# The last norm of a trunk layer: roots one step ahead of the scaling, one quarter row on ScalarE and GpSimd

## The chip, the cores and the metric

The kernel runs on one core of a Trainium2 chip. The metric is the device time of one execution in microseconds (us), as the median of three runs. The engines are named as the profile names them: PE (TensorE matmul), PEld (its weight loads), DVE (VectorE), ACT (ScalarE), POOL (GpSimd) and SP (SyncE, which issues DMAs). A small q behind a name is the engine's sequencer: issues, waits, drains.

## The reference

One layer of an encoder trunk on 512 tokens of 1024 channels: a mixing sub-layer (recurrent branch, attention branch, merge, norm, residual), and a feed-forward sub-layer. Only the end of the second one matters here:

```python
def rms_norm(x, gain):
    y = xf * lax.rsqrt(jnp.mean(xf * xf, axis=-1, keepdims=True) + RMS_EPS)
    return y * gain
...
ffn_out = jnp.einsum("bsf,fd->bsd", jax.nn.gelu(gate) * val, w_down[layer])
x = x + rms_norm(ffn_out, ffn_norm_post[layer])
```

For each token: the sum of squares of its 1024 outputs of the down projection, the reciprocal root of it (the "factor"), and output = product with gain, times factor, plus residual.

## The kernel before

All matrix products are float32 made of two parts: each operand is cast to a high part (ScalarE) and the rest is its low part (VectorE, a subtraction of two operands in SBUF), and three matmuls multiply high by high, high by low and low by high.

**The down projection** is done as seven products of half-size blocks (a scheme with fewer products than eight). Each product n has six steps, so there are 42 steps, in the order of products 1, 4, 5, 6, 7, 3, 2. Step i does this, in an order that is written out by hand (`manual_schedule`, nothing is reordered by a planner; every engine takes its instructions in this order):

- `load_w(i + 5)`: SyncE loads the weights of a later step.
- `down_step(i)`: the matmuls of step i, for two tiles of 128 tokens (t = 0, 1) and 512 columns, into PSUM banks `slot[n][t]`.
- `prep(i + 2)`: the casts (ScalarE, `wh_dn` and `ah`) and splits (VectorE, `wl_dn` and `al`) for step i + 2, out of rings of four buffers.
- `extra[i]`: whatever else is put into that step, the last norm's work among it. `at_[n]` is the first step of product n: 30 for product 3, 36 for product 2.

**The tokens** are four tiles of 128 (t = 0 to 3). Tiles 2 and 3 need products that are complete after step 29; tiles 0 and 1 need all of them. The matmuls of the last four steps (38 to 41) are put behind all preparations, and go by tile: tile 0 for the four steps, then tile 1's columns 0 to 255 (`X`), then 256 to 511 (`Y`).

**The norm of tiles 2 and 3** stands in `extra` of the steps from 30 on. For each of the two halves of a row, one step folds the PSUM result with a kept partial sum (VectorE, `fold`, L1671), the next squares and sums it (ScalarE, `square`, L1678) and multiplies with the gain into `os[t]` (VectorE, `gained`, L1681). Then one step does both of these:

- `scale_of`: root on ScalarE (L269), reciprocal on VectorE (L271);
- `finish_by_dma`: ScalarE scales the whole row, 128x1024 (L1699), GpSimd issues a DMA that adds the residual (L1700, `accum_op`), and a DMA puts the row out (L1701), for tile 2 from GpSimd's queue, for tile 3 from SyncE's.

Tile 2 has the steps 30 to 34, tile 3 the steps 34 to 38. Step 38 is the first whose matmuls come late, so its `extra` runs behind all preparations.

**The norm of tiles 0 and 1** has its second half (columns 512 to 1023) folded, squared and multiplied in steps 38 and 39. The rest follows the last matmuls: `fold_part` (L1759, L1760: fold on VectorE, square on ScalarE), `gained_part` (L1763), `rest_end` (L263, which adds two of the partial sums of squares), and `finish` (L1694, L1696): VectorE computes scale times row plus residual in one instruction, and a DMA puts the piece out.

A DMA queue issues in order: SyncE's queue holds tile 3's output first, then the pieces of tiles 0 and 1.

Of the kernel before, what the change touches and what calls it, by code (L numbers as in the profile page):

```python
# [11 lines left out]
AF = mybir.ActivationFunctionType  # L12
ALU = mybir.AluOpType
# [84 lines left out]
def kernel(  # L98
# [15 lines left out]
    nc = tc.nc  # L114
    act, dve, pool, pe = nc.scalar, nc.vector, nc.gpsimd, nc.tensor
# [11 lines left out]
    ov = out.rearrange("(t p) d -> p t d", p=P)  # L127

    HALVES = (slice(0, 512), slice(512, 1024))
# [131 lines left out]
    def rest_of(name, parts, eps=EPS):  # L261
        rest = small.tile([P, 1], F32, tag="ss", name=f"rest_{name}")
        dve.tensor_scalar(out=rest, in0=parts[0], scalar1=eps, scalar2=parts[1] if len(parts) > 1 else None, op0=ALU.add,  # L263
                          **({"op1": ALU.add} if len(parts) > 1 else {}))
        return rest

    def rstd_of(part, name, rest=epst):
        sd = small.tile([P, 1], F32, tag="sd", name=f"sd_{name}")
        act.activation(out=sd, in_=part, func=AF.Sqrt, bias=rest)  # L269
        rs = small.tile([P, 1], F32, tag="rs", name=f"rs_{name}")  # L270
        dve.reciprocal(rs, sd)  # L271
        return rs
# [85 lines left out]
    X, Y = slice(0, SH), slice(SH, S)  # L358
# [172 lines left out]
    with ExitStack() as rg:  # L531
        rt, ixt, tt = {}, {}, {}
        last_act = [None]
        with ExitStack() as r0:
# [69 lines left out]
            with tc.tile_pool(name="pre", bufs=2, side="right", reuse_waits="tile") as pre, ExitStack() as wp:  # L604
# [80 lines left out]
                for c in HALVES:  # L685
                    pool.tensor_tensor(out=us[0].wl[:, c], in0=us[0].raw[:, c], in1=us[0].wh[:, c].bitcast(F32),
                                       op=ALU.subtract)
# [363 lines left out]
    with ExitStack() as at:  # L1051
# [165 lines left out]
        i = KD - 2  # L1217
# [37 lines left out]
    x2t = xpool.tile([P, NT, D], F32, name="x2t")  # L1255
# [323 lines left out]
    with man2:  # L1579
# [90 lines left out]
        def fold(i, t, ps):  # L1670
            dve.tensor_tensor(out=kept[i][t], in0=ps, in1=kept[i][t], op=ALU.add)  # L1671

        s2o = {t: dpool.tile([P, 3], F32, name=f"s2_o{t}", bufs=1) for t in range(NT)}
        os = [dpool.tile([P, D], F32, name=f"o{t}") for t in range(NT)]
        junk = dpool.tile([P, DH], F32, name="junk")

        def square(t, h, src):
            act.activation(out=junk, in_=src, func=AF.Square, scale=ROOT, accum_out=s2o[t][:, h : h + 1])  # L1678

        def gained(t, h, src):  # L1680
            dve.tensor_tensor(out=os[t][:, HALVES[h]], in0=src, in1=gpost[:, HALVES[h]], op=ALU.mult)  # L1681

        rso = {}
# [3 lines left out]
        def rest_end(t, *cols):  # L1687
            rest_o[t] = rest_of(f"o{t}", [s2o[t][:, i : i + 1] for i in cols])

        def scale_of(t, c=0):  # L1690
            rso[t] = rstd_of(s2o[t][:, c : c + 1], f"o{t}", rest_o[t])

        def finish(t, c, queue):
            dve.scalar_tensor_tensor(out=os[t][:, c], in0=os[t][:, c], scalar=rso[t], in1=x2t[:, t, c],  # L1694
                                     op0=ALU.mult, op1=ALU.add)
            queue.dma_start(ov[:, t, c], os[t][:, c])  # L1696

        def finish_by_dma(t, queue):
            act.activation(out=os[t], in_=os[t], func=AF.Copy, scale=rso[t])  # L1699
            nc.gpsimd.dma_start(os[t], x2d[t * P : (t + 1) * P], accum_op=ALU.add)  # L1700
            queue.dma_start(ov[:, t], os[t])  # L1701

        extra = {i: [] for i in range(len(STEPS))}
        at_ = {n: NS * PRODUCTS.index(n) for n in PRODUCTS}
# [18 lines left out]
        for t in range(2):  # L1723
            todo = []
            for h, n in ((1, 5), (0, 4)):
                todo += [lambda t=t, n=n: fold(n, t, slot[1][t]),
                         lambda t=t, h=h, n=n: (square(2 + t, h, kept[n][t]), gained(2 + t, h, kept[n][t])) + ((rest_end(2 + t, 1),) if h else ())]
            todo.append(lambda t=t: (scale_of(2 + t), finish_by_dma(2 + t, (nc.gpsimd, nc.sync)[t])))
            for i, f in enumerate(todo):
                extra[at_[3] + 4 * t + i].append(f)  # L1730
        for t in range(2):
            a = at_[2] + 2 + t
            extra[a].append(lambda t=t: fold(6, t, slot[5][t]))
# [24 lines left out]
        def fold_part(t, c, i):  # L1758
            dve.tensor_tensor(out=kept[1][t][:, c], in0=slot[2][t][c.start // SH][:, c] if t else slot[2][t], in1=kept[1][t][:, c], op=ALU.add)  # L1759
            act.activation(out=junk[:, c], in_=kept[1][t][:, c], func=AF.Square, scale=ROOT, accum_out=s2o[t][:, i : i + 1])  # L1760

        def gained_part(t, c):
            dve.tensor_tensor(out=os[t][:, c], in0=kept[1][t][:, c], in1=gpost[:, c], op=ALU.mult)  # L1763
# [3 lines left out]
        scale_of(0)  # L1767
        fold_part(1, X, 0)
        finish(0, HALVES[1], nc.sync)
        gained_part(1, X)  # L1770
        rest_end(1, 0, 1)
        fold_part(1, Y, 2)
        gained_part(1, Y)
        scale_of(1, 2)
        finish(0, HALVES[0], nc.sync)
        finish(1, HALVES[1], nc.sync)
        finish(1, X, act)
        finish(1, Y, nc.sync)


_INS = ["x", "gains", "cp", "w_in", "w_f", "rgw", "w_proj_a", "w_proj_b", "w_out", "w_up", "w_down"]
# [86 lines left out]
```

## Time and profile before

| what | before |
|---|---|
| median of three runs | 875.69 us (875.36 to 876.43) |
| profiled execution, its own time | 875.8 us |
| its span, first to last instruction | 873.9 us |
| granted TensorE clock, mean | 0.997 |
| last matmul starts, PE | 866.14 us |
| reciprocal of tile 1, DVE | 867.78 us |
| last output DMA issued, SP | 870.07 us |

The profiled execution's own time is 1.9 us more than its span. In a timeline row the first number is the start in us from the span's start, the second the duration; a row with x2 or more is several instructions that follow one another, merged, with the shape of the first. In square brackets stands how long the engine was idle before it, and what ended that wait. In a chain or a list of waits, "A <- B: total, times, longest" means that A waited for B. In a group's row, the numbers behind the bar are busy us and the mean ns of one.

### The profile page before, as it was taken

To read this page: it belongs to the slowest core of one execution; us is meant where nothing else is said; L and a number is where in the kernel's file an instruction comes from. 1 tells how busy PE (TensorE), PEld (TensorE's weight loads), DVE (VectorE), ACT (ScalarE), POOL (GpSimd) and SP (SyncE) were. 2 spreads that over 40 slices of the span, in tenths; PEclk is the share of its full clock that TensorE was granted. 3 is DMA by queue.
4 is the path that set the end of the run, shared out by engine and by line. 5 is a ranking of instruction groups with operands and counts; after the bars stand their busy time and mean duration, and the time that the engine had idled before them with its cause. 6 is when DMAs were issued, how large, how long until landed. Compare 5 with 4: busy or idle time off the path is not lost.

```text
span 873.9 us, 15792 instructions
## 1 busy us (share of the span) xinstructions
PE 864.5 (99%) x5856; PEld 793.1 (91%) x5856; DVE 734.8 (84%) x1209; ACT 598.9 (69%) x1031; POOL 229.7 (26%) x282
## 2 busy tenths in 40 slices
PE   9999999999999999999999999999999999999996
PEld 7888888888899998888888889999999999988885
DVE  7998469774578859999868699999999999889997
ACT  7556595543466657776755496888888888678664
POOL 4244534454111033323205100233233233100000
PEclk9999999999999999999999999999999999999998
DMA  7777689979965478354606662789999988699875
GB/s 267 227 252 215 203 218 251 268 205 246 229 164 151 121 233 286 111 175 153 230 26 205 220 212 100 148 208 248 260 241 257 230 212 216 209 392 353 299 224 159
DMA packets 72256, 188.38 MB, mean 216 GB/s; under 512 B 7601, under 2 KB 28129, under 8 KB 71794
## 3 DMA queue, kind: packets, MB, share of 16 engines
q1 hardware_dynamic: 48576, 130.86, 44.6%
q0 software_dynamic: 23456, 56.37, 30.3%
q8 instruction: 46, 0.75, 0.3%
q14 instruction: 32, 0.26, 0.1%
q10 hardware_dynamic: 146, 0.14, 0.1%
HBM read 152.79 MB, written 37.83 MB: 218 GB/s over the span
## 4 chain that ended last, share of the span: by engine, by line
PE 91%; DVE 5%; issue 2%; ACT 1%; DMA 0%; DVEq 0%; ACTq 0%
PE dn L1564 7%; PE up L459 7%; PE up L462 7%; PE up L460 7%; PE av L1133 2%; PE pa L242 2%; PE ga L244 2%; PE ga L243 2%; PE pa L244 2%; PE pa L243 2%; PE ga L242 2%; PE wo L1275 2%; PE pb L242 2%; PE xa L242 2%; PE wo L1276 2%
## 5 line engine op out<-in xcount | busy, mean ns | idle before, releaser
L1434 DVE SCALAR_TENSOR_TENSOR u<-up,cft,u 128x511 f32<-128x511 f32 x96 | 71.3, 745 | 3.5 <-ACT u L1428 1.8
L395 POOL DMA_DIRECT2D ml<-raw_up x42 | 36.1, 860 | 144.3 <-ACT ml L394 84.8
L459 PE MATMUL up<-sh,th 128*128 128x256 f32 x252 | 59.6, 275 | 0.2 <-DVE up L478 0.2
L460 PE MATMUL up<-sl,th 128*128 128x256 f32 x252 | 59.5, 275 | 0.0
L196 ACT CAST wh_dn<-raw_dn 128x1024 fp32r<-128x1024 f32 x42 | 43.9, 1045 | 17.8 <-DMA raw_dn<-td 12.3
L199 DVE TENSOR_TENSOR wl_dn<-raw_dn,wh_dn 128x1024 fp32r<-128x1024 f32 x42 | 51.1, 1217 | 4.7 <-ACT wh_dn L196 4.7
L355 DVE TENSOR_TENSOR tl<-t,th 128x1024 fp32r<-128x1024 f32 x42 | 51.3, 1221 | 0.0
L1428 ACT ACTIVATE u<-up,cft 128x512 f32<-128x512 f32 x48 | 37.0, 780 | 20.7 <-PE up L462 9.6
L459 PEld LDWEIGHTS up<-sh,th 128*128 128x128 f32 x252 | 48.4, 192 | 0.4 <-DVE up L478 0.4
L460 PEld LDWEIGHTS up<-sl,th 128*128 128x128 f32 x252 | 48.4, 192 | 0.0
L1442 POOL TENSOR_TENSOR yf<-u,u 128x512 f32<-128x512 f32 x23 | 30.7, 1333 | 61.7 <-issue 46.1
L441 ACT CAST th<-t 128x1024 fp32r<-128x1024 f32 x42 | 43.7, 1043 | 3.0 <-DVE t L355 0.7
L1564 PE MATMUL dn<-wh_dn,al 128*128 128x512 f32 (+1 forms) x180 | 45.0, 366 | 0.0
L1564 PE MATMUL dn<-wl_dn,ah 128*128 128x512 f32 (+1 forms) x180 | 44.9, 365 | 0.0
L1564 PE MATMUL dn<-wh_dn,ah 128*128 128x512 f32 (+1 forms) x180 | 44.8, 365 | 0.0
L971 POOL TENSOR_TENSOR B<-B,mask 128x128 f32<-128x128 f32 x64 | 30.2, 500 | 37.6 <-DMA B<-cnd 37.6
L459 PE MATMUL up<-h2h,mh 128*128 128x256 f32 x168 | 39.7, 275 | 0.0
L460 PE MATMUL up<-h2l,mh 128*128 128x256 f32 x168 | 39.7, 275 | 0.0
L462 PE MATMUL up<-sh,tl 128*128 128x256 f32 x252 | 38.4, 275 | 0.0
L1564 PEld LDWEIGHTS dn<-wh_dn,al 128*128 128x128 f32 x180 | 32.9, 189 | 4.4 <-DVE al L355 0.3
L1564 PEld LDWEIGHTS dn<-wl_dn,ah 128*128 128x128 f32 x180 | 32.9, 189 | 4.3 <-DVE wl_dn L199 0.2
L1564 PEld LDWEIGHTS dn<-wh_dn,ah 128*128 128x128 f32 x180 | 32.9, 189 | 4.2
(742 smaller groups left out, 3209.5 us busy)
## 6 DMA issues: line engine op xcount, KB each, us to landing
raw_up<-in_w_up_dram SPq DMA_DIRECT2D x48, 512.0 KB, 5.3
td<-in_w_down_dram POOLq DMA_DIRECT2D x36, 512.0 KB, 6.0
raw_dn<-td SPq DMA_DIRECT2D x24, 512.0 KB, 6.1
ml<-raw_up POOLq DMA_DIRECT2D x21, 512.0 KB, 5.4
B<-cnd POOLq DMA_DIRECT2D x16, 640.0 KB, 5.7
raw_dn<-in_w_down_dram SPq DMA_DIRECT2D x18, 512.0 KB, 4.6
raw_wo<-in_w_out_dram SPq DMA_DIRECT2D x16, 512.0 KB, 4.5
td<-td POOLq DMA_DIRECT2D x12, 512.0 KB, 12.6
```

What stands on the lines that cost most here:

```text
L196: act.copy(self.wh, self.raw)
L199: engine.tensor_tensor(out=self.wl, in0=self.raw, in1=self.wh.bitcast(F32), op=ALU.subtract)
L242: pe.matmul(dst, ah, bh, start=first, stop=False)
L355: dve.tensor_tensor(out=out, in0=a, in1=b, op=ALU.subtract)
L395: nc.gpsimd.dma_start(l, src, accum_op=ALU.add)
L441: act.copy(self.th[i], self.t[i])
L459: pe.matmul(dst, wh[:, k], turns(ah[:, k]), start=first and k == 0, stop=False, skip_group_check=True)
L460: pe.matmul(dst, wh[:, k], turns(al[:, k]), start=False, stop=False, skip_group_check=True)
L462: pe.matmul(dst, wl[:, k], turns(ah[:, k]), start=False, stop=k == KH - 1, skip_group_check=True)
L1428: act.activation(out=c, in_=ps, func=AF.Identity, scale=fcol(C_CFW + 3 * e + 2), bias=fcol(C_CFB + e))
L1434: dve.scalar_tensor_tensor(out=c[:, s:], in0=ps[:, : S - s], scalar=fcol(C_CFW + 3 * e + j), in1=c[:, s:], op0=ALU.mult, op1=ALU.add)
L1564: pe.matmul(d[:, x], y[:, k, tok], turns(w[:, k], SH)[:, h], start=fresh and m == kind == k == 0, stop=m == NS - 1 and kind == 2 and k == ...
```

## The change

It touches two places. In the norm of tiles 2 and 3, root and reciprocal become a step of their own, with the scaling and its DMAs one step behind; tile 3's steps begin three steps behind tile 2's, not four. So tile 2 has the steps 30 to 35 (root in 34, scaling in 35), tile 3 the steps 33 to 38 (root in 37, scaling in 38).

Behind the last matmuls, tile 0's first half is finished right behind its second one, in front of tile 1's last fold; `rest_end` and both products of tile 1's first half go behind that fold; and the last quarter row `X` of tile 1 is scaled on ScalarE and gets its residual on GpSimd, while VectorE finishes the second half and the quarter `Y`. `Y` is put out from ScalarE's queue, `X` from SyncE's.

```diff
             for h, n in ((1, 5), (0, 4)):
                 todo += [lambda t=t, n=n: fold(n, t, slot[1][t]),
                          lambda t=t, h=h, n=n: (square(2 + t, h, kept[n][t]), gained(2 + t, h, kept[n][t])) + ((rest_end(2 + t, 1),) if h else ())]
-            todo.append(lambda t=t: (scale_of(2 + t), finish_by_dma(2 + t, (nc.gpsimd, nc.sync)[t])))
+            todo.append(lambda t=t: scale_of(2 + t))
+            todo.append(lambda t=t: finish_by_dma(2 + t, (nc.gpsimd, nc.sync)[t]))
             for i, f in enumerate(todo):
-                extra[at_[3] + 4 * t + i].append(f)
+                extra[at_[3] + 3 * t + i].append(f)
...
         scale_of(0)
         fold_part(1, X, 0)
         finish(0, HALVES[1], nc.sync)
+        finish(0, HALVES[0], nc.sync)
+        fold_part(1, Y, 2)
+        rest_end(1, 0, 1)
         gained_part(1, X)
-        rest_end(1, 0, 1)
-        fold_part(1, Y, 2)
         gained_part(1, Y)
         scale_of(1, 2)
-        finish(0, HALVES[0], nc.sync)
+        act.activation(out=os[1][:, X], in_=os[1][:, X], func=AF.Copy, scale=rso[1])
+        pool.tensor_tensor(out=os[1][:, X], in0=os[1][:, X], in1=x2t[:, 1, X], op=ALU.add)
         finish(1, HALVES[1], nc.sync)
-        finish(1, X, act)
-        finish(1, Y, nc.sync)
+        finish(1, Y, act)
+        nc.sync.dma_start(ov[:, 1, X], os[1][:, X])
```

## The prediction

> **What bounds the kernel now.** I read the page first, then the waits of the last 94 us, then the timeline of the last 16 us engine by engine, then the DMA windows behind the last matmul.
>
> ```profile
> span 873.9 us, 15792 instructions
> PE 864.5 (99%) x5856; PEld 793.1 (91%) x5856; DVE 734.8 (84%) x1209; ACT 598.9 (69%) x1031; POOL 229.7 (26%) x282
> ```
>
> TensorE is busy 99% of the span, so a change that adds no matmul and removes none can win in two places only: where TensorE is held up, and behind its last matmul. The waits from 780 us on:
>
> ```profile
> ACT o L1699 <- DVE rs_o L271: 3.7, 2, 2.0
> ```
> ```profile
> SPq L1701 <- DMA o<-x2d: 16.1, 1, 16.1
> ```
>
> ScalarE stands still for 3.7 us in two waits, because a tile's square root and its scaling are in one step: the scaling waits for a reciprocal that stands on VectorE behind two long splits. SyncE's queue (last row, from the waits of its queue) stands 16.1 us for tile 3's residual add. The timeline shows what each costs (ScalarE, VectorE, TensorE, in turn):
>
> ```profile
> 857.62 0.61 ACT L1525 CAST ah<-q 128x512 fp32r<-128x512 f32 x1
> ```
> ```profile
> 860.41 1.15 ACT L1699 ACTIVATE o<-o,rs_o 128x1024 f32<-128x1024 f32 x1 [1.98 <-DVE rs_o L271]
> ```
> ```profile
> 849.66 1.23 DVE L199 TENSOR_TENSOR wl_dn<-raw_dn,wh_dn 128x1024 fp32r<-128x1024 f32 x1 [1.62 <-ACT wh_dn L196]
> 859.62 0.68 DVE L355 TENSOR_TENSOR al<-q,ah 128x512 fp32r<-128x512 f32 x1
> 860.22 0.15 DVE L271 RECIPROCAL rs_o<-sd_o 128x1 f32<-128x1 f32 x1
> ```
> ```profile
> 859.37 0.59 PE L1564 MATMUL dn<-wh_dn,ah 128*128 128x512 f32 x2
> 859.80 0.65 PE L1564 MATMUL dn<-wl_dn,ah 128*128 128x512 f32 x2
> 860.36 0.70 PE L1564 MATMUL dn<-wh_dn,al 128*128 128x512 f32 x2
> 860.89 0.27 PE L1564 MATMUL dn<-wh_dn,ah 128*128 128x256 f32 x1
> ```
>
> Tile 2's stall makes the next cast late and VectorE idle for 1.62 us, its only idle time in this stretch. VectorE never makes that up: the last split, al at 859.62 to 860.30, comes when TensorE already waits. Pairs of matmuls start 0.43 us apart (859.37 to 859.80), but the next two take 0.56 and 0.53: TensorE loses 0.13 + 0.10, say 0.22 us. Behind the last matmul:
>
> ```profile
> 866.02 0.39 PE L1564 MATMUL dn<-wh_dn,al 128*128 128x256 f32 x2
> ```
> ```profile
> 865.26 0.74 DVE L1694 SCALAR_TENSOR_TENSOR o<-o,rs_o,x2t 128x512 f32<-128x512 f32 x1
> 865.92 0.42 DVE L1763 TENSOR_TENSOR o<-kept,gpost 128x256 f32<-128x256 f32 x1
> 866.25 0.21 DVE L263 TENSOR_SCALAR rest_o<-s_o 128x1 f32<-128x1 f32 x1
> 866.45 0.42 DVE L1759 TENSOR_TENSOR kept<-dn,kept 128x256 f32<-128x256 f32 x1
> ```
> ```profile
> 867.78 0.16 DVE L271 RECIPROCAL rs_o<-sd_o 128x1 f32<-128x1 f32 x1 [0.44 <-ACT sd_o L269]
> 867.86 2.19 DVE L1694 SCALAR_TENSOR_TENSOR o<-o,rs_o,x2t 128x512 f32<-128x512 f32 x4
> ```
> ```profile
> 867.45 0.34 SPq L1701 DMA_DIRECT2D out_dram<-o  x1
> ```
> ```profile
> 868.62 0.48 SPq L1696 DMA_DIRECT2D out_dram<-o  x1
> ```
> ```profile
> 870.07 0.39 SPq L1696 DMA_DIRECT2D out_dram<-o  x1
> ```
>
> TensorE ends at 866.41, the last fold begins at 866.45 and tile 1's reciprocal at 867.78, 1.33 later. Then four scalings, in one merged row of 2.19 us (867.86 to 870.05), the last issue at 870.07. But SyncE got tile 3 away only at 867.45, so all of tiles 3, 0 and 1 (1536 KB) leaves behind that:
>
> ```profile
> 867.45:868.28 0.83, 0.00 (x0) 0.00 (x0) 0.50 (x2) 0.29 (x1) 0.00 (x0) 1.00 0.00 0
> 868.28:869.75 1.47, 0.00 (x0) 0.00 (x0) 1.47 (x4) 0.00 (x0) 0.00 (x0) 0.92 0.99 387
> 869.75:872.57 2.82, 0.00 (x0) 0.00 (x0) 0.29 (x1) 0.00 (x0) 0.00 (x0) 0.50 0.99 356
> 872.57:873.94 1.37, 0.00 (x0) 0.00 (x0) 0.00 (x0) 0.00 (x0) 0.00 (x0) 0.50 0.00 0
> ```
>
> In these windows the last two columns are the DMA engines' busy share and GB/s. Nothing moves for 0.83 us behind the first issue; then the engines are 99% busy until 872.57; then 1.37 us of landing and closing. So the end is set by a DMA backlog: 1536 KB at 356 to 387 GB/s, behind a first issue that waited for tile 3.
>
> **The change, part by part.**
>
> *Factors a step ahead of the scaling.* The instructions are the same; order moves. With the root and reciprocal in steps 34 and 37 and the scalings in 35 and 38, each reciprocal has passed on VectorE before ScalarE comes to the scaling. Queued behind the stalled scaling were ScalarE's next casts, and behind them VectorE's splits. Removing the stall gives VectorE up to 1.62 us; I take all of it, since fold, square and product of tile 3 only move one step and each finds its input ready (the sums that they fold are complete from step 30 on). The last al then ends at 858.7 against TensorE's need at about 860.2: the 0.22 us of TensorE is won, with 1.5 us to spare. Bounds: 0 (the stall reappears) to 0.22. Worth 0.22.
>
> *Tile 3.* Its scaling directly follows the last cast. That ends at 858.23 now, and some 1.2 us sooner when ScalarE no longer starts late (it cannot go much further: the buffers come free when TensorE ends step 37, the row below). So the scaling runs from 857.0 to 858.2, not from 860.41 to 861.56.
>
> ```profile
> 855.48 0.38 PE L1564 MATMUL dn<-wh_dn,ah 128*128 128x512 f32 x1
> ```
> ```profile
> 861.85 0.86 POOL L1700 DMA_DIRECT2D o<-x2d  x1 [6.54 <-ACT o L1699]
> ```
> ```profile
> DMA to landing us min/median/max: 2.8/2.9/5.5
> ```
>
> The add was issued 0.29 us behind the scaling (861.85) and landed 5.5 us later; now it is issued at 858.5 and lands at 864.0. SyncE's queue is free at 864.0, not at 867.4, and tile 3's 512 KB and the two halves of tile 0 leave behind TensorE's last 2 us, before 867.5. This is the large part: at the end only tile 1's 512 KB is left.
>
> *Tile 0's second half scaled before the last fold.* One scaling (0.66 us start to start, 865.26 to 865.92) goes from behind the reciprocal to in front of the fold; a product (0.33) and a sum (0.20) go behind the fold. With the lead of 1.62 us, that chain ends near 865.2, and VectorE waits for TensorE (866.19) with 1.0 us in hand: cost nothing. Without the lead the fold begins at 865.92 + 0.66 = 866.58, which is 0.13 late. Behind the fold the sum and two products take 0.33 + 0.20 + 0.33 + 0.42 = 1.28 us, and the reciprocal comes at 1.33: hidden with 0.05 to spare, bounds 0 to 0.1.
>
> *One quarter on ScalarE and GpSimd.* The trace has no such pair. For the ScalarE scaling of 128x256 the nearest row is the square of that size, for the GpSimd add the two sizes on either side:
>
> ```profile
> L1760 ACT ACTIVATE junk<-kept 128x256 f32<-128x256 f32 x2 | 0.8, 417 | 1.6 <-DVE kept L1759 1.6
> ```
> ```profile
> L1442 POOL TENSOR_TENSOR yf<-u,u 128x512 f32<-128x512 f32 x23 | 30.7, 1333 | 61.7 <-issue 46.1 <-ACT u L1438 8.7 <-DVE t L355 3.6
> L971 POOL TENSOR_TENSOR B<-B,mask 128x128 f32<-128x128 f32 x64 | 30.2, 500 | 37.6 <-DMA B<-cnd 37.6
> ```
>
> So 0.42 us, and between 0.50 and 1.33 for the add; on the straight line between them 0.78. With 0.2 us from reciprocal to ScalarE (860.22 to 860.41 for tile 3) and 0.1 for each hand-over, the quarter is issued at R + 0.2 + 0.42 + 0.1 + 0.78 + 0.1 = R + 1.6, where R is the start of the reciprocal (bounds R + 1.3 to R + 2.2). VectorE meanwhile scales 512 and then 256 columns, done at R + 1.2.
>
> A GpSimd operation beside a VectorE operation with two SBUF inputs is in the trace:
>
> ```profile
> 757.32 1.22 DVE L199 TENSOR_TENSOR wl_dn<-raw_dn,wh_dn 128x1024 fp32r<-128x1024 f32 x1
> 758.45 1.78 DVE L355 TENSOR_TENSOR al<-yr,ah 128x512 fp32r<-128x512 f32 x1
> ```
> ```profile
> 757.47 2.22 POOL L1442 TENSOR_TENSOR yf<-u,u 128x512 f32<-128x512 f32 x1 [7.36 <-issue]
> ```
>
> GpSimd's add took 2.22 instead of 1.33 and ended 1.15 behind VectorE's split; VectorE's next split took 1.78 instead of 0.68 and ended 0.54 behind GpSimd's add. They took turns. At the end the same happens: VectorE's 512 columns first, GpSimd's add to about R + 1.5, VectorE's last 256 done at about R + 1.9. The Trainium skill (SBUF — State Buffer, "SBUF: two separate sides") states this as a lock: the port pair that VectorE and GpSimd share is held for a whole instruction by whichever starts first, and the other blocks. The trace agrees: 1.15 and 0.54 behind the other's end. By the lock the quarter given to GpSimd saves VectorE almost nothing (R + 1.9 for its last columns); without it both are through by R + 1.6.
>
> *The sum.* R = 867.78 - 0.22 = 867.56. The 512-column scaling starts 0.08 later, its DMA 0.76 behind that start (867.86 to 868.62): 868.40. First data 0.83 later: 869.23. From there 512 KB: 1.35 us at 387 GB/s, 1.47 at 356; the pieces are small and the engines do not all begin at once, so I take 1.55: 870.78. The two quarters are issued at 868.8 and 869.2 (869.5 if they take turns) and their data stands ready at 869.6 to 870.3, before the queue has emptied, so the order of GpSimd and VectorE hardly shows. Then 1.37 to the end: 872.15, against 873.94. The gain is 1.79 us: 0.22 from TensorE, the rest from the backlog. The profiled execution took 875.8 by its own time, 1.9 more than its span; the median of the three runs is 875.69, so 873.9. Bounds of the parts: without TensorE's 0.22 and with the sum late by 0.1 and the data at 1.7, 874.4; with 1.35 for the data, 873.7.
>
> **Rivals.**
>
> *A DMA's own time takes over.* The small DMAs issued at the end took 2.8 and 2.9 us to land, though I read that as backlog:
>
> ```profile
> out_dram<-o ACTq DMA_DIRECT2D x1, 128.0 KB, 2.9
> out_dram<-o SPq DMA_DIRECT2D x1, 128.0 KB, 2.8
> ```
>
> If 2.8 is their price in a quiet queue too, the last issue at 869.16 lands at 871.96, where it was 872.87: a gain of 0.9, 874.8. For it: the 512 KB of tile 2, with little beside it, took 2.9 also. Against it: 0.83 + 0.34 of data + 0.3 of landing is 1.5.
>
> *GpSimd late.* If the add starts late and also takes turns, the quarter is issued at R + 2.2 = 869.76, data from 870.6 to 871.1, end 872.5: 874.2.
>
> *The lead doesn't come*, because something else holds ScalarE or VectorE in steps 33 to 38: fold at 866.58, everything behind it 0.35 later than forecast, 874.25; the backlog still shrinks as long as tile 3 lands before 867.
>
> *Slower: GpSimd's closing drain.* GpSimd ends the program by draining:
>
> ```profile
> L1864 POOLq DRAIN  x3: 51/93/7927, 861.8 to 873.7; - x3
> ```
>
> The first of the three at the end began at 861.8, beside the last add's issue, and lasted 7.9 us, to 869.8, hidden. Now it begins behind the quarter's add, at about 869.1. If it takes 7.9 there, it ends at 877.0 and with some 0.7 of closing the span is 877.7: 879.5. It decides once the drain exceeds 2.2 us. Against it: 7.9 is probably the work of the DMA issued beside it, done long before; the others took 0.05 and 0.09.
>
> **How the numbers follow.** Forecast 0.62 (873.4 to 874.4, likeliest 873.9); DMA's own time 0.15 (874.8); GpSimd late 0.08 (874.2); no lead 0.08 (874.25); drain 0.05 (879.5); nothing left of it 0.02 (875.7). The range 873.2 to 874.9 leaves out the drain and the last, and some of the edges. Differences within 0.2% (1.75 us) are about what a measurement of this kernel can tell from no change, and the forecast lies on that edge: faster by more has 0.68 of the forecast's share and a little of the late cases, 0.45; within 0.2% the rest, 0.48; slower the drain and a remainder, 0.07.
>
> **What would show it.** Right: no wait of ScalarE's L1699 for the reciprocal; pairs of matmuls 0.43 apart up to 860.9; tile 3's output issued near 864; the DMA engines idle shortly before 869, then about 1.5 us of data; GpSimd's add between VectorE's last two scalings. Wrong: an issue near 869.2 that lands at 872 (own time), a last issue beyond 869.7 (GpSimd), a last fold behind 866.4 (no lead), a drain of several us ending last.

## The result, and the profile after

| | before | after |
|---|---|---|
| median | 875.62 us (874.82 to 877.38, 22 runs) | 877.97 us (875.91 to 879.86, 22 runs) |
| profiled execution, its own time | 875.8 us | 876.66 us |
| its span | 873.9 us | 874.9 us |
| start of tile 1's last fold | 866.45 us | 866.45 us |
| SyncE's queue through with its last output | 873.17 us | 871.85 us |
| end of the drain on GpSimd | 869.76 us | 874.10 us |

The ratio is 1.0024 (95%: 1.0019 to 1.003): slower, by 2.1 us by the ratio, where 873.9 was forecast. A second measurement gave 876.80 against 875.94, ratio 1.0012 (1.0003 to 1.0021). Both intervals lie above 1, so both say slower, by 0.1 to 0.2%; how much is taken up below.

The page of the changed kernel: the busy time of TensorE is what it was, the span is 1.0 us longer.

```profile
span 874.9 us, 15794 instructions
PE 864.5 (99%) x5856; PEld 793.5 (91%) x5856; DVE 733.8 (84%) x1208; ACT 599.1 (68%) x1032; POOL 229.2 (26%) x283
```

The timeline of TensorE at the place where pairs of matmuls came 0.56 and 0.53 us apart:

```profile
859.60 0.60 PE L1564 MATMUL dn<-wh_dn,ah 128*128 128x512 f32 x2
860.03 0.59 PE L1564 MATMUL dn<-wl_dn,ah 128*128 128x512 f32 x2
860.46 0.59 PE L1564 MATMUL dn<-wh_dn,al 128*128 128x512 f32 x2
860.90 0.38 PE L1564 MATMUL dn<-wh_dn,ah 128*128 128x256 f32 x2
```

They now come 0.43, 0.43 and 0.44 apart. This execution is 0.23 us late on arrival (859.60 against 859.37) and level with the one before at the last row (860.90 against 860.89): the stall of 0.22 us is gone. That the last fold starts at 866.45 in both is the sum of the two.

The timelines of GpSimd and of SyncE's queue:

```profile
857.27 0.56 POOL L1701 DMA_DIRECT2D out_dram<-o  x1 [6.39 <-DMA o<-x2d]
858.83 0.86 POOL L1700 DMA_DIRECT2D o<-x2d  x1 [1.00 <-ACT o L1699]
868.57 0.74 POOL L1778 TENSOR_TENSOR o<-o,x2t 128x256 f32<-128x256 f32 x1 [8.88 <-ACT o L1777]
```
```profile
865.80 0.34 SPq L1701 DMA_DIRECT2D out_dram<-o  x1
866.20 2.90 SPq L1696 DMA_DIRECT2D out_dram<-o  x3
869.34 0.33 SPq L1781 DMA_DIRECT2D out_dram<-o  x1
```

Tile 3's add is issued at 858.83 instead of 861.85, and its output leaves at 865.80 instead of 867.45. The new GpSimd add runs from 868.57 to 869.31, and the last issue on SyncE's queue is at 869.34, where it was 870.07 (the last of all is now ScalarE's, at 869.63). VectorE and ScalarE behind the last matmul:

```profile
866.45 0.42 DVE L1760 TENSOR_TENSOR kept<-dn,kept 128x256 f32<-128x256 f32 x1 [0.94 <-PE dn L1564]
867.78 0.16 DVE L271 RECIPROCAL rs_o<-sd_o 128x1 f32<-128x1 f32 x1
867.98 1.62 DVE L1694 SCALAR_TENSOR_TENSOR o<-o,rs_o,x2t 128x512 f32<-128x512 f32 x2
```
```profile
867.98 0.51 ACT L1777 ACTIVATE o<-o,rs_o 128x256 f32<-128x256 f32 x1 [0.23 <-DVE rs_o L271]
869.63 0.38 ACTq L1696 DMA_DIRECT2D out_dram<-o  x1
```

VectorE waits 0.94 us for TensorE ahead of the fold, and ends its last scaling at 869.60, not 870.05. So every engine but GpSimd is earlier or level. The DMA windows (last two columns: busy share of the DMA engines, GB/s; the column before them is the granted clock):

```profile
866.62:868.76 2.14, 0.00 (x0) 0.00 (x0) 1.99 (x7) 1.31 (x4) 0.19 (x1) 1.00 1.00 388
868.76:869.60 0.84, 0.00 (x0) 0.00 (x0) 0.84 (x1) 0.00 (x0) 0.55 (x1) 1.00 0.71 268
869.60:871.18 1.58, 0.00 (x0) 0.00 (x0) 0.00 (x0) 0.00 (x0) 0.00 (x0) 0.65 0.94 328
871.18:874.89 3.71, 0.00 (x0) 0.00 (x0) 0.00 (x0) 0.00 (x0) 0.00 (x0) 0.50 0.00 0
```

The last data moves at 871.18, 1.39 us sooner than before (872.57). But from there to the end it takes 3.71 us with nothing at work on any engine or DMA, where it took 1.37. The chain of waits does not say why: its last pieces (start, us) are VectorE's and end at 869.59.

```profile
867.98 0.75 DVE o L1694
868.73 0.86 DVEq L1867
```

The answer is in the group of the last line, where the sequencers' own instructions stand (min, median and max in ns, first and last start):

```profile
L1867 POOLq DRAIN  x3: 51/93/5568, 868.5 to 874.6; - x3
L1867 SPq DRAIN  x3: 7/7/7, 871.8 to 874.4; - x3
```

SyncE is through with the last output at 871.85. GpSimd's drain, which begins with its last operation (868.53), lasts 5.57 us, to 874.10: 4.78 behind the end of the add. Everything else then waits for it. Before, the drain lasted 7.93 but began at 861.83 and was over at 869.76, behind other work.

### The profile page after: what moved, and what is told of

Same layout as the page of the kernel before. It is cut to its first block, busy times and chain, and to the rows that moved or that the text cites. A ratio compares the mean times of both kernels' runs of the same rounds, so it can differ in the third digit from the quotient of the medians.

```text
span 874.9 us, 15794 instructions
## 1 busy us (share of the span) xinstructions
PE 864.5 (99%) x5856; PEld 793.5 (91%) x5856; DVE 733.8 (84%) x1208; ACT 599.1 (68%) x1032; POOL 229.2 (26%) x283
## 4 chain that ended last, share of the span: by engine, by line
PE 97%; DVE 1%; ACT 1%; DMA 1%; issue 0%; POOL 0%; DVEq 0%; ACTq 0%; POOLq 0%
PE dn L1564 13%; PE up L459 8%; PE up L460 8%; PE up L462 7%; PE av L1133 2%; PE ga L244 2%; PE ga L243 2%; PE ga L242 2%; PE pa L242 2%; PE pa L243 2%; PE pa L244 2%; PE wo L1275 2%; PE pb L242 2%; PE xa L242 2%; PE v L339 2%; PE wo L1276 2%
```

## The experiments

Executions differ by 1 to 4 us in what happens hundreds of us ahead of the change (the last fold starts anywhere from 865.49 to 869.43 us in the profiles). So each profile is also read from the start of tile 1's last fold to the end of the span ("fold to end"): 7.49 us before, 8.43 after, 8.43 again in a second profile of the changed kernel.

### What the closing drain costs, and for what

**The change without the GpSimd add** (`e1_no_pool`): the quarter `X` goes back to VectorE, with its residual.

```diff
-        act.activation(out=os[1][:, X], in_=os[1][:, X], func=AF.Copy, scale=rso[1])
-        pool.tensor_tensor(out=os[1][:, X], in0=os[1][:, X], in1=x2t[:, 1, X], op=ALU.add)
         finish(1, HALVES[1], nc.sync)
         finish(1, Y, act)
-        nc.sync.dma_start(ov[:, 1, X], os[1][:, X])
+        finish(1, X, nc.sync)
```

**The kernel before with a tiny GpSimd copy at the end** (`e2_before_tiny`): 128x1 from tile 1's last quarter, behind its scaling.

```diff
         finish(1, Y, nc.sync)
+        pool.tensor_copy(out=tick, in_=os[1][:, 511:512])
```

**The change without the last GpSimd DMAs** (`e3_no_swdge`): the residual adds of tiles 2 and 3 are left out, and tile 2 goes out by SyncE.

```diff
             act.activation(out=os[t], in_=os[t], func=AF.Copy, scale=rso[t])
-            nc.gpsimd.dma_start(os[t], x2d[t * P : (t + 1) * P], accum_op=ALU.add)
             queue.dma_start(ov[:, t], os[t])
```

> The changed kernel with the quarter row X of tile 1 scaled on VectorE again, behind Y, and put out from SyncE: no ScalarE scaling and no GpSimd add at the end, all else as changed. Theory D (GpSimd's closing drain sets the end: 5.57 us from 868.53 to 874.10 in the changed kernel, while SyncE was through at 871.85): GpSimd's last work is then the residual add of tile 3, issued near 858.8, its drain ends near 867 and is hidden; the end is SyncE's, near 871.8 plus 0.75 of closing: span 872.5, a time of 874.3, 1.3 us below before. Rival O (the reordering itself loses, the drain only fills what would be waited anyway): span stays at 874 to 875, a time at or above before. A drain of GpSimd that still ends beyond 871 would speak against D as I put it.

> The kernel before with one GpSimd copy of 128x1 behind its last scaling, and nothing else. Theory D (the drain costs some 4.8 us from the end of GpSimd's last operation, whatever that is): the copy ends near 870.3, the drain near 875.1, closing to 875.9: 2.0 us slower than before. Rival T (the 4.8 us belong to the add of 128x256, its size or its kind): the drain is below 1 us, ends by 871.5 and is hidden, same time as before. Rival S (the drain waits for the work of the last DMA that GpSimd issued, near 861.9, done by 869.8): same time as before.

> The changed kernel without the two residual adds by DMA that GpSimd issues for tiles 2 and 3 (the residual of these two tiles is left out, and tile 2 goes out from SyncE's queue); GpSimd's add of the quarter X stays. GpSimd's last DMA is then some 100 us earlier. Theory D (a fixed cost behind the last operation): the drain is again 4.5 to 5.6 us, ends near 874, span near 874.9, time 876.5 to 878. Rival S (the drain is what a DMA issued shortly before leaves behind on GpSimd): the drain is below 1 us, SyncE ends last near 871.6, span 872.4, time 874.2.

| | median us, ratio to before (95%) | GpSimd's last operation ends | drain ends | fold to end |
|---|---|---|---|---|
| without the add | 875.27, 0.9994 (0.9982 to 1.0005) | 862.15 (a DMA's issue) | 869.15, hidden | 6.09 |
| before + copy | 877.92, 1.0021 (1.0012 to 1.0031) | 871.81 (copy 128x1) | 876.59, +4.78 | 9.41 |
| without the DMAs | 876.29, 1.0006 (0.9997 to 1.0014) | 872.32 (add 128x256) | 876.86, +4.54 | 8.21 |

The group of the last line without the add:

```profile
L1865 POOLq DRAIN  x3: 51/93/7886, 861.3 to 873.3; - x3
L1865 SPq DRAIN  x3: 7/7/7, 872.8 to 873.1; - x3
```

Here the drain is over long before SyncE, and the tail has nearly the length that was forecast: 6.09 us from the fold, where 5.92 was forecast. The median gains less, 0.6 us where the expectation had 1.3; a part of that is taken up under the late weight load. The timeline and the last line's group of the kernel before with the copy added:

```profile
871.62 0.18 POOL L1779 COPY tick<-o 128x1 f32<-128x1 f32 x1 [7.39 <-DVE o L1694]
```
```profile
L1865 POOLq DRAIN  x3: 51/93/4987, 871.6 to 877.1; - x3
```

In the kernel before, a copy of 0.18 us costs 1.92 us of fold to end (9.41 against 7.49), and the drain is as long behind it as behind the add: 4.78. So neither a copy or an add nor its size sets it. And with the last GpSimd DMA some 100 us away, it is nearly the same, 4.54:

```profile
L1866 POOLq DRAIN  x3: 46/102/5288, 871.6 to 877.4; - x3
```

(The median of this last version, 876.29, hardly differs from before; it also leaves out two adds of 512 KB, so it is the drain in its profile that is read here, not its time.)

Behind a computing instruction the drain is thus not the tail of a DMA issued beside it, but a price of its own. Where GpSimd's last instruction is the issue of tile 3's add, it is different. The drain's row and SyncE's issue of tile 3's output, which waits for that add, without the GpSimd add and with the steps alone (`e4_steps_only`, below):

```profile
866.84 0.34 SPq L1701 DMA_DIRECT2D out_dram<-o  x1
```
```profile
L1865 POOLq DRAIN  x3: 51/93/8057, 857.8 to 871.9; - x3
```
```profile
863.59 0.34 SPq L1701 DMA_DIRECT2D out_dram<-o  x1
```

The drains end at 869.15 and 865.90, both 2.31 us behind SyncE's issue. The same stands in all eight profiles in which GpSimd's work ends with this issue (2.31 in six of them, the kernel before among them with 867.45 to 869.76, and 2.27 in two of a gated version below), while from the end of the add's issue to the end of the drain it is anything from 6.98 to 7.52. So such a drain also waits until its DMA has landed. That it ends 2.31 us behind and not 4.78 suggests that a part of its own work passes while the DMA is under way; this was not shown.

### What sets its length

Six programs without the layer (it is left out; the input goes to the output by way of SBUF) do some DMAs on GpSimd, 27 us or more in which GpSimd has nothing to do, and then a 128x1 copy on GpSimd. They differ in the DMAs that GpSimd issues; the first two also have more ScalarE copies in between, and the second a memset on GpSimd. There is one profiled execution of each. In outline:

```python
    for i in range(100):        # none; 1 (a load from DRAM); 100; 100 with accum_op; 50; 100 of 16 rows
        nc.gpsimd.dma_start(got[i % 4], xt[:, i % 4])
    ...
    pool.tensor_copy(out=mark, in_=work[:, 0:1])
```

> The drain by itself: a kernel that leaves the whole layer out (it copies x to the output through SBUF), with 40 ScalarE copies of 128x1024 and one GpSimd copy of 128x1 behind them as GpSimd's last operation; GpSimd issues no DMA. Theory D1 (any last GpSimd operation costs some 4.8 us of closing drain): a drain of 4.5 to 5 us behind the copy. Theory D2 (only a program whose GpSimd has issued DMAs pays it): a drain below 0.3 us, like the 0.19 us drain at the start of the kernel before.

> The same with one GpSimd memset and one 512 KB load issued by GpSimd some 40 us ahead of its last operation. D1: the same drain of 4.5 to 5 us. D2: 4.5 to 5 us here, against below 0.3 without the DMA.

> The small kernel again (it leaves the layer out and copies x to the output), now with 100 DMAs of 512 KB from SBUF to SBUF issued by GpSimd, then ScalarE copies and one GpSimd copy of 128x1 as GpSimd's last operation. If the drain grows with the number of DMAs that GpSimd has issued: 3 to 5 us (the kernel before issues about 170). If not: 0.3 us, as with none and with one.

> As m3_swdge_100, but the 100 DMAs add to what is there. If adding DMAs leave the work behind: 3 to 5 us here and 0.3 in m3_swdge_100. If it is neither the number nor the adding: 0.3 us in both, and what makes the drain long in the full kernel stays open.

> The layer is left out, as in the programs before it: GpSimd issues 50 DMAs of 128x1024 floats from one SBUF buffer to another (100 in the program before, whose closing drain ended 8.26 us behind GpSimd's last copy; with one DMA it was 0.15, with none 0.06), then all is idle until a last 128x1 copy on GpSimd. If the drain does a piece of work for each DMA that GpSimd issued in the program (N, a count): 50 times 0.082 = 4.1 us behind the copy. If it is a step that many DMAs switch on (N2, a flat cost): about 8.3, as with 100. If only the last few matter (N3): well below 4.1.

> The layer is left out: 100 GpSimd DMAs again, but each of 16 rows of 1024 floats and not 128, an eighth of the bytes and of the rows. If the closing drain works per DMA (N): 8.3 us behind the last copy, as with full rows. If it works per row, packet or byte (B): about 1.0 to 1.1 us (8.26 / 8). The layer's kernel, whose three counts 118, 117 and 115 gave 4.78, 4.70 and 4.54, has pieces of several sizes, so B would let its 118 DMAs cost less than 8.3; under N that stays unexplained.

The group of the last line of each, in this order (none, 1, 100, 100 accumulating, 50, 100 of 16 rows):

```profile
L223 POOLq DRAIN  x3: 34/70/272, 45.5 to 46.2; - x3
```
```profile
L227 POOLq DRAIN  x3: 34/82/362, 46.6 to 47.5; - x3
```
```profile
L230 POOLq DRAIN  x3: 34/95/8457, 173.7 to 182.6; - x3
```
```profile
L230 POOLq DRAIN  x3: 34/95/6295, 304.9 to 311.7; - x3
```
```profile
L230 POOLq DRAIN  x3: 34/95/4374, 109.0 to 113.9; - x3
```
```profile
L230 POOLq DRAIN  x3: 34/95/8457, 115.7 to 124.7; - x3
```

Each drain begins 0.02 to 0.03 us before the copy of 0.18, so it ends 0.07, 0.16, 8.25, 6.09, 4.17 and 8.25 us behind the copy. (The expectations have 0.06, 0.15 and 8.26 for the first three, by rounded rows.) Both readings tried first, 4.5 to 5 us for any program and the same as soon as GpSimd has issued one DMA, fell with the first two programs, and the 3 to 5 us expected of 100 DMAs were too little. The rows fit 0.07 plus 0.082 us for each DMA that GpSimd issued in the program (4.17 for 50 where 4.1 was expected of a count, and 8.3 of a flat cost), or 0.060 for each accumulating one. An eighth of the rows and bytes changes nothing: 8.25 again. The last DMA had long landed (GpSimd waited 28 us for the copy's input in the third), so this is no transfer that is still under way, and an idle GpSimd does not do it ahead of time.

The layer's kernels agree in the difference. By the counts of the view of DMA issues, the kernels before and after issue 118 from GpSimd, the versions below with tile 2's output on SyncE's queue 117, the one without the adds 115; the drains behind the last computing instruction are 4.78, 4.70 and 4.54: 0.08 for each, though two of the three that the last leaves out are accumulating. (The expectation of m3_swdge_100 has about 170 for 118.) They do not agree in the sum: 118 at 0.082 would be 9.7 us, at 0.060 still 7.1. Some DMAs of the layer are not charged at its end; which, and why, was not tried.

### The two halves of the change

**The steps alone** (`e4_steps_only`): the first hunk of the change on the kernel before. **The tail alone** (`e5_tail_only`): the second hunk, with `X` on VectorE as above, and the steps of before.

> The kernel before with the first half of the change alone: root one step ahead of the scaling, tile 3's steps three behind tile 2's; the end behind the last matmuls as before. Theory: TensorE gets its 0.22 us, tile 3 leaves near 865.8 instead of 867.45, and the DMA backlog at the end shrinks to 768 KB from 869.2 on: data to 871.5, span 872.8, time 874.5, 1.1 us faster. Rival O (reordering loses or wins nothing): 875.6 or more.

> The other half alone: the order behind the last matmuls as in the change but with the quarter X on VectorE (no GpSimd add), and the steps of tiles 2 and 3 as before. Backlog reading: tile 3 still leaves only near 867.5, so 1536 KB go out behind it as before, data to 872.5; the scaling that is taken from behind the reciprocal is worth nothing and the fold is 0.13 later at most: 875.6 to 876.0, the same as before. Rival (the scalings on VectorE set the end, not the backlog): 0.6 to 0.7 us faster, 875.1.

| | median us, ratio to before (95%) | tile 3 out (SyncE), from the fold | last output issued, from the fold | fold to end |
|---|---|---|---|---|
| before | | +1.00 | +3.62 | 7.49 |
| steps alone | 875.60, 0.9994 (0.9985 to 1.0002) | -1.90 | +3.63 | 6.64 |
| tail alone | 875.93, 1.0004 (0.9995 to 1.0013) | +0.79 | +3.21 | 7.30 |
| both, no GpSimd add | 875.27, 0.9994 (0.9982 to 1.0005) | -0.66 | +3.09 | 6.09 |

The tail alone issues its last output 0.41 us sooner and wins 0.19 from the fold; but its fold starts 0.18 us behind TensorE's end (867.84 to 868.02), where it was 0.04 before, so only 0.05 is left. The steps alone issue it no sooner and win 0.85. So the backlog behind tile 3 set the end, as the prediction read it, and an earlier last issue is worth something only once tile 3 is out of the way (both together win 1.40). The medians are too close to before to tell these apart, and that of the steps alone misses its expectation, 874.5, by 1.1 us; it is the profiles, one of each, that tell.

### A weight load that comes late

In the profile of `e1_no_pool` TensorE stalls just where the change was to free it: its timeline, the wait of ScalarE (its timeline), and the DMAs issued from 849.6 to 860 (KB, us to landing):

```profile
858.74 0.59 PE L1564 MATMUL dn<-wh_dn,al 128*128 128x512 f32 x2
860.00 0.70 PE L1564 MATMUL dn<-wh_dn,ah 128*128 128x512 f32 x2 [0.66 <-ACT ah L1525]
```
```profile
858.38 1.04 ACT L196 CAST wh_dn<-raw_dn 128x1024 fp32r<-128x1024 f32 x1 [3.61 <-DMA raw_dn<-in_w_down_dram]
```
```profile
o<-x2d POOLq DMA_DIRECT2D x1, 512.0 KB, 8.9
raw_dn<-in_w_down_dram SPq DMA_DIRECT2D x1, 512.0 KB, 8.6
```

The pairs are 1.26 us apart instead of 0.43, because the last weights took 8.6 us to land beside tile 2's residual add, which is now issued within 0.06 us of them (at 849.61 and 849.67; in the kernel before at 848.99 and 850.92, the add 1.9 us ahead). In the profile of the changed kernel (850.02 and 850.09) the same load took 4.4, so the meeting alone does not make it late. To take the meeting away, tile 2's add was put behind the landing of these weights (`e7_after_gate`), and the same was done without the final GpSimd add (`e6_no_pool_gate`):

```diff
+        def residual_by_dma(t, gate=None):
+            if gate is not None:
+                pool.tensor_copy(out=tick, in_=wd[gate].raw[:, 0:1])
             nc.gpsimd.dma_start(os[t], x2d[t * P : (t + 1) * P], accum_op=ALU.add)
-            queue.dma_start(ov[:, t], os[t])
+            nc.sync.dma_start(ov[:, t], os[t])
...
+            extra[(36, 38)[t]].append(lambda t=t: residual_by_dma(2 + t, (41, None)[t]))
```

The scalings stay in steps 35 and 38. The edit also moves tile 2's output from GpSimd's queue to SyncE's, so what it does is not the gate's alone. Each was measured twice, beside further measurements of the change and of the change without the add.

> The kernel without the GpSimd add (as e1_no_pool), and in addition tile 2's residual add is held back on GpSimd until the last weight load (step 41) has landed, by a GpSimd copy of one column of that load; both outputs of tiles 2 and 3 go out from SyncE. Theory C (in the changed kernel tile 2's add and the last weight load are issued within 0.1 us, at 849.6 to 850.1, share the DMA engines, and in some executions the load lands late: 858.3 in the profile of e1_no_pool, where TensorE then stood 1.3 us; before, the add was 1.9 us ahead of the load and the load landed at 855.8): the load lands by 855, TensorE never waits near 859, the median is 0.6 to 1.0 us below e1's repeat, near 874.3. Without C (the late load of that profile was chance, and no more frequent than before): the same as e1's repeat, within 0.4 us.

> The changed kernel, its GpSimd add of the quarter X included, with tile 2's residual add held back until the last weight load has landed, as in e6_no_pool_gate. Theory D plus C: what is left is the drain, 0.9 us of loss (fold to end 8.4 us against 7.5): 876.5 to 876.9, against 877.9 of the changed kernel. Theory D alone, with the rest of the loss from elsewhere: 877.5 to 878.

> e1_no_pool again, beside the others on the same chip: near 875.3, 0.6 below before, with single executions from 873.4 to 878.6. Theory C: the profile shows the last weight load landing anywhere from 854.5 to 858.5, and a wait of TensorE near 859 whenever it is beyond about 857.

> The changed kernel again, beside the three others on one chip. Theory D (the drain alone: fold to end 8.4 us against 7.5 before): 0.9 us above before. Theory D plus C (the late weight load in a part of the executions adds to it): 1.5 to 2.2 us above before, as in its first measurement, and clearly above e7b.

> e7_after_gate again (the changed kernel, tile 2's residual add held back until the last weight load has landed). D plus C: 0.8 to 1.2 us above before, and 0.6 us or more below after2. D alone: the same as after2 within 0.4 us.

> e1_no_pool a third time (no GpSimd add): fold to end 6.05 us against 7.5, so 1.4 us below before without C; 0.6 to 1.0 below with C. Against after2 2.35 us less in either case, since both have the same steps ahead.

> e6_no_pool_gate again: 1.4 us below before. C: 0.4 us or more below e1c; without C: the same as e1c.

| | median us, ratio to before (95%) | late load | fold to end |
|---|---|---|---|
| the change, second measurement | 876.80, 1.0012 (1.0003 to 1.0021) | no | 8.43 |
| the change, gated | 877.03, 1.0014 (1.0005 to 1.0022) | no | 8.35 |
| again | 876.62, 1.0005 (0.9996 to 1.0013) | no | 8.34 |
| without the add, second | 874.53, 0.9984 (0.9975 to 0.9993) | yes | 6.10 |
| without the add, third | 875.12, 0.9988 (0.9979 to 0.9997) | no | 6.11 |
| without the add, gated | 874.67, 0.9988 (0.9979 to 0.9997) | no | 6.05 |
| again | 874.44, 0.9981 (0.9972 to 0.9990) | no | 6.02 |

The timeline of GpSimd in the last version: the copy of 1.84 us is the gate, the add goes out behind it.

```profile
853.69 1.84 POOL L1703 COPY tick<-raw_dn 128x1 f32<-128x1 f32 x1 [83.31 <-DMA raw_dn<-in_w_down_dram]
855.47 0.85 POOL L1704 DMA_DIRECT2D o<-x2d  x1
858.98 0.87 POOL L1704 DMA_DIRECT2D o<-x2d  x1 [2.66 <-ACT o L1699]
```

The load was late (8.6 and 8.4 us) in two of the six profiles with the steps moved, the residual adds kept and no gate, took 4.2 to 5.8 in the other four, and was late in none of the four with the gate. So few profiles do not show that the gate did it. What it is worth in the median is not settled either: side by side, the gate won 0.7 us (875.12 and 874.44), 0.2 (876.80 and 876.62) and nothing (874.53 and 874.67), where the expectations had 0.4 or more, 0.6 or more, and 0.6 to 1.0.

With both halves of the change in place, the GpSimd add separates the versions at each measurement: without it, 874.4 to 875.3; with it, 876.6 to 878.0 (876.3 where the residual adds were left out as well). Without the add, the median is 0.6, 1.2 and 0.8 us below the kernel before without the gate, and 1.0 and 1.5 with it.

## Why the prediction was wrong

**The rival on GpSimd's closing drain decided it.** It had the place (behind the quarter's add, at 869.1; in fact 869.31) and, nearly, the point from which it decides (over 2.2 us behind it; SyncE was through 2.54 behind it, at 871.85). The step that failed is its price: "7.9 is probably the work of the DMA issued beside it, done long before; the others took 0.05 and 0.09", and with it the chance of 0.05. The runs showed 4.78 us behind the add, 4.78 behind a copy of 128x1, and 4.54 with no GpSimd DMA for some 100 us. Half of the reading holds: the drain of 7.93 before does end by the DMA beside it, 2.31 us behind SyncE's issue that waits for its landing. What does not follow is that little is left of the drain where no DMA stands beside it. The trace of before, with a single long drain, behind a DMA, could not tell the two apart.

In the sum: forecast from fold (866.23) to end (872.15), 5.92 us. Without the GpSimd add it measured 6.02 to 6.11 in five profiles, against 7.49 before. With the add 8.43. So the add with the drain behind it cost 2.3 us, all of the gain and 0.94 more.

**What stood.** *TensorE's 0.22*: won, by the rows above. *The lead*: VectorE waits 0.94 us ahead of the last fold (forecast 1.0), so tile 0's second half in front of it costs nothing; sum and products lie behind it and the reciprocal comes 1.33 later, as before. *The quarter*: the add took 0.74 us (0.78 estimated), ScalarE's scaling 0.51 (0.42), the issue came at R + 1.56 (forecast R + 1.6). *Taking turns*: VectorE's last 256 columns ended at 869.60, R + 1.82 (forecast R + 1.9); the wait was paid on VectorE's side, whose 256 columns ended 0.29 behind the add and took twice their time (0.95 by the trace, 0.48 without GpSimd), while the add, at 0.74, shows none. *The last data*: 1.58 us from 869.60 (forecast 1.55 from 869.23), up to 871.18 (forecast 870.78, on an execution 0.23 earlier, and with the first scaling 0.08 behind the start of the reciprocal where it was 0.20). So GpSimd late and no lead fell as rivals.

**What the quarter was worth.** The prediction said that by the lock it saves VectorE almost nothing, but did not set it against leaving `X` on VectorE. In the version without the GpSimd add VectorE scales all three pieces itself:

```profile
868.82 0.16 DVE L271 RECIPROCAL rs_o<-sd_o 128x1 f32<-128x1 f32 x1
869.02 1.54 DVE L1694 SCALAR_TENSOR_TENSOR o<-o,rs_o,x2t 128x512 f32<-128x512 f32 x3
```

It is through at R + 1.74, 0.08 sooner than with two pieces beside GpSimd's add, and its last output is issued 3.09 us behind the fold, not 3.18. So handing the quarter to ScalarE and GpSimd gained nothing even before the drain is counted.

**What stood only in part.** *Tile 3* left at 865.80, not near 864.0: its add was issued 0.3 later than forecast and took 6.9 us to land, not 5.5. Tile 2's output now stands only 1.6 us ahead of it on the same queue (857.27; before, 7.1 us ahead, at 854.75), but that does not explain it: in the second profile of the changed kernel the output stands 1.1 us ahead (857.70 and 858.84), and the add took 5.8, as long as in the gated versions, where that output is not on this queue (5.7 to 6.0). Why it took 6.9 once stays open. The lead on the backlog was large enough all the same. *A DMA's own time*: the two last issues of the changed kernel took less than 2.8 to land,

```profile
out_dram<-o SPq DMA_DIRECT2D x1, 128.0 KB, 1.8
out_dram<-o ACTq DMA_DIRECT2D x1, 128.0 KB, 1.9
```

so the 2.8 and 2.9 of before were backlog, as argued. The other profiles agree: the last two issues take 1.8 to 2.1 us wherever tile 3 has left before the last fold, and 2.7 to 3.1 where it leaves behind it. The own time is nearer to 1.8 than to the 1.5 that was added up.

**What was left out.** The prediction followed tile 3's add and only the reciprocal of tile 2. Tile 2's scaling moves one step back, from 34 to 35, its add with it (850.02, not 848.99), while the last weight load comes 0.8 us sooner (850.09, not 850.92): the two meet. Where the load then came late, TensorE's pairs stood 0.83 us further apart (1.26 against 0.43), more than the 0.22 that the change wins there.

**What stays open.** From fold to end and TensorE's 0.22 together, the change should cost 0.94 - 0.22 = 0.7 us; by the ratios the second measurement says 1.1 (0.3 to 1.8), the first 2.1 (1.7 to 2.6), which leaves out 0.7. The version without the add falls short in the same way: 1.40 won behind the fold, 0.6 to 1.2 in the median. Late loads in some executions would fit the difference; this was not shown. Nor is it known what the drain still does in the 2.31 us behind a landing. Nor is it known why the layer's 118 DMAs cost less at the end than 118 in a row.

## What to carry to other kernels

An engine that has long been idle is not free to use at the end: look at what it has hidden. Here GpSimd's closing drain lay under the last matmuls and outputs as long as GpSimd's last instruction came early; a computing instruction put behind them, an add of 128x256 or a copy of 128x1, brings 4.8 us of it to the end. So give GpSimd its last work early, or have few DMAs issued from it. Ask also what the engine that is to be relieved would have needed for the piece itself: here VectorE was through no later when it kept the piece. And when a step is moved, ask of every DMA that it issues which other transfer it meets at its new time.

## What the runs showed that was not expected

- In the programs without the layer, the drain on GpSimd lasts 0.082 us for each DMA that GpSimd issued in the program, whether of 512 or 64 KB (50: 4.17, 100: 8.25, 100 of an eighth: 8.25), 0.060 for each accumulating one (100: 6.09), 0.07 with none; it comes at the end, though the engine stood idle for 28 us just before. In the layer it is 4.78 us for 118. The Trainium skill (VectorE: DVE Perf Modes, "The DRAIN you can't avoid") gives about 12 ns as a constant for the drains at the beginning and end of a program on all engines. The short ones of these traces (7 ns on SyncE, 8 on TensorE's weight loads in the programs without the layer) agree in size, GpSimd's does not.
- Where GpSimd's last instruction issues a DMA, its drain ends 2.27 to 2.31 us behind SyncE's issue that waits for that DMA's landing, in all eight profiles.
- Two transfers of 512 KB issued within 0.06 us of one another, a weight load and an accumulating add from GpSimd, took 8.6 and 8.9 us in one profile and 8.4 and 8.6 in another; in four others, issued as close (0.04 to 0.07 us), the load took 4.2 to 5.8.
